# A third query tile, output weights split ahead of time, and later turning of weights in a two-layer streaming encoder

## The chip, the cores and the metric

The kernel runs on one core of a Trainium2 chip. The metric is the device time of one execution in microseconds (us); lower is better. The tensor engine (PE) multiplies, the vector (DVE), scalar (ACT) and GpSimd (POOL) engines do everything elementwise, and the sync engine (SP) issues nearly all DMAs, in the order of its own queue.

## What is computed

A prompt of 2048 frames and a sample of 64 frames with caches, model width 1024, 16 heads of 64. Layer one: RMSNorm, one projection to q, k, v and gate, softmax attention over a band of nine chunks of 64 frames, gate, output projection, residual. Then one shared k and v for layer two: stick-breaking attention (strictly causal, a running product instead of a softmax), gate, output projection, residual, final RMSNorm.

```python
# layer one, per chunk of 64 queries
s = einsum(q, k) * SCALE + rel_bias;  p = softmax(where(mask, s, NEG_INF));  o = p @ v
xp = xp + (o * silu(gate)) @ w_out_a
# layer two, per block of 128 queries, over all earlier keys
z = einsum(q, k) * SCALE
log_fail = where(mask, log_sigmoid(-z), 0)
later = flip(cumsum(flip(log_fail))) - log_fail
w = where(mask, exp(log_sigmoid(z) + later), 0);  o = w @ v
xp = xp + (o * silu(gate)) @ w_out_b
y = rms_norm(xp, norm_f)
```

## The kernel before, in words

Everything is float32. To keep precision on PE, an operand is split in a high part `hi` (rounded, on ACT) and the rest `lo` (on DVE), and a product is made of two or three matmuls: the helper `split`. Nearly every instruction is issued through one recording helper, so the profile gives them line L90; here they are told apart by the tiles they write and read.

The program has four stages, one after the other.

1. First projections (`projections("a", ...)`): `ps_v` and `ps_t` are their PSUM tiles. Beside them a list of small *stages* runs, a few per job: caches are turned and split and put into DRAM in the layout that the attention wants.
2. First attention, in *beats* (class `Beat`). One beat makes the scores `z` of one query tile of 128; two beats after the last tile of an item (`LAG["a"]`) its weights `s` are turned on PE (`wt`), split into `ph` and `pl`, and one beat later (`HOLD`) multiplied with v into `acc`. Between the beats, at `RATE` 0.4 steps a beat, goes work that fills PE: late projection jobs (`ps_j`, for the second half of the prompt), the splitting of the output weights (`w_out_steps`, which gives PE nothing), the output projection (`ps_o`).
3. Second projections, with stages of their own (`staged_b`): differences of v, and cached keys `kr` that are turned, split to `kh`, `kl` and stored in `k_b`.
4. Second attention, in beats again, `LAG` 5, `HOLD` 2, `RATE` 0.3. ACT makes `f` from `z`, POOL makes products of pairs (`two`), DVE scans them into `s` tiles (10 of them), POOL fills in the values between, then PE turns them. Per pair of heads the first half of the items has four query loads `q` (groups 1 and 0, two heads each): items of 8, 8, 4 and 4 beats, and a sample item of 2. `q` has two buffers, `kt` and `vt` (keys and values) five each.

In the beats most instructions aren't pinned: a scheduler at build time decides the place of each in its engine's queue, from the order in which the program gives them, buffers and its own estimate of times. Loads go through `Queue.load`, which makes a load stand behind the oldest store that was given at least 24 beats before it:

```python
behind = self.stores and self.stores[0][0] <= self.clock - self.pace
with tc.issue_after(self.stores[0][1].ins) if behind else nullcontext():
    nc.sync.dma_start(out, in_)
```

In a late k job of the first attention, `out` splits a chunk into `sp` and stores it (`k_a`), `add_back` adds the two parts on POOL into `lkn`, and `token_rows` turns `lkn` on PE (`ps_r`) for the output. `sp` and `lkn` share two buffers.

Of the kernel before, what the change touches and what calls it, by code (L numbers as in the profile page):

```python
# [9 lines left out]
F32 = mybir.dt.float32  # L10
F32R = mybir.dt.float32r
# [5 lines left out]
P = 128  # L17
D = 1024
NK = D // P
# [13 lines left out]
CH = 512  # L33
# [9 lines left out]
KEPT = "b"  # L43

RATE = dict(a=0.4, b=0.3)
LAG = dict(a=2, b=5)

LEAD = dict(a=8, b=14)
HOLD = dict(a=1, b=2)
# [21 lines left out]
def f32(ap):  # L71
    return ap.bitcast(F32)
# [28 lines left out]
def encoder_step(ctx: ExitStack, tc: tile.TileContext, a: dict, o: dict):  # L101
    nc = tc.nc
# [4 lines left out]
    def in_place(what):  # L107


        def pinned():  # L110
            was, order.on = order.on, order.amid
            what()
            order.on = was

        return pinned

    sp = order.engine(nc.sync)

    class Queue:


        def __init__(self, pace):
            self.pace, self.clock, self.stores = pace, 0, []

        def store(self, out, in_):
            self.stores.append((self.clock, nc.sync.dma_start(out, in_)))
# [1 line left out]
        def load(self, out, in_):  # L128
            while len(self.stores) > 1 and self.stores[1][0] <= self.clock - self.pace:
                self.stores.pop(0)  # L130
            behind = self.stores and self.stores[0][0] <= self.clock - self.pace
            with tc.issue_after(self.stores[0][1].ins) if behind else nullcontext():
                nc.sync.dma_start(out, in_)  # L133

# [3 lines left out]
    queue = Queue(24)  # L138
# [16 lines left out]
    def big_pair():  # L155
        return [big.tile([P, NK, D], F32R, name=f"big{i}", tag=f"big{i}") for i in range(2)]
# [28 lines left out]

    vraw = dram.tile([1 + T, D], F32, name="v_raw")
    x1d = dram.tile([T, D], F32, name="x1")
    biasd = [dram.tile([P, 2, 640], F32, name=f"bias_{i}") for i in range(HP)]
    relx = dram.tile([H, 384], F32, name="relx")

# [15 lines left out]
    def split(hi, lo, src):  # L206
        act.activation(hi, src, AF.Copy)
        dve.tensor_tensor(lo, src, f32(hi), ALU.subtract)
# [271 lines left out]
        nc.sync.dma_start(f32(lay["b"]["v"][to : to + n, heads]), f32(vs[:n]).rearrange("p h s d -> p h (s d)"))  # L480


    def stage_bias(hp, pool):
        for h in range(2):
            toe = pool.tile([P, 256], F32, name="toe", tag="toe", bufs=1)
            row = relx[2 * hp + h : 2 * hp + h + 1, 1:257]
            nc.sync.dma_start(toe, bass.AP(tensor=row.tensor, offset=row.offset, ap=[[1, P], [1, 256]]))
            bt = pool.tile([P, 640], F32, name="bt", tag="bt", bufs=1)
            dve.tensor_scalar(bt[:, 384:640], toe[:, ::-1], 8.0, None, ALU.mult)

            dve.tensor_scalar(bt[:, 0:384], toe[:, 255:256].to_broadcast([P, 384]), 8.0, None, ALU.mult)
            dve.memset(bt[DH:P, 0:DH], NEG8)
            dve.memset(bt[0:DH, 640 - DH : 640], NEG8)
            nc.sync.dma_start(biasd[hp][:, h], bt)
# [15 lines left out]
    def load_q(L, pool, hp, h, q0):  # L510

        there(L, "q", hp, q0)
        q = pool.tile([P, 2, CH], F32R, name="q", tag="q", bufs=3 if L == "a" else 2)
        src = f32(lay[L]["q"][hp][:, h * DH : h * DH + DH, place(q0) : place(q0) + CH]).rearrange("s d t -> d s t")
        for s in range(2):
            queue.load(f32(q[s * DH : s * DH + DH]), src[:, s : s + 2])
        return q
# [206 lines left out]
    def late_job(L, kind, w, c0, g, hp, x2, first, prompt):  # L724
        st = {}

        def load():
            if L not in KEPT:
                st["raw"] = opool.tile([P, NK, P], F32, name="lraw", tag="og", bufs=1)
                c = c0 + hp * P  # L730
                sp.dma_start(st["raw"], w[:, c : c + P].rearrange("(k p) c -> p k c", p=P))
            st["wh"] = opool.tile([P, NK, P], F32R, name="lwh", tag="oh", bufs=2)
            st["wl"] = opool.tile([P, NK, P], F32R, name="lwl", tag="ol", bufs=2)
            if L in KEPT:
                for i, part in enumerate((st["wh"], st["wl"])):
                    sp.dma_start(f32(part), f32(lay[L]["w"][kind, hp][i]))

        def cut(k0):
            ks = slice(k0, k0 + STEP)
            scaled_split(st["wh"][:, ks], st["wl"][:, ks], st["raw"][:, ks], g[:, ks])  # L740

        def some(c, k0):
            if k0 == 0:
                st["ps"] = bank("ps_j")
            ps, wh, wl = st["ps"], st["wh"], st["wl"]
            cols = slice(c, c + CH)
            for k in range(k0, k0 + STEP):
                mm(ps, wh[:, k], x2[0][:, k, cols], start=(k == 0), stop=False)
                mm(ps, wh[:, k], x2[1][:, k, cols], start=False, stop=False)
                mm(ps, wl[:, k], x2[0][:, k, cols], start=False, stop=(k == NK - 1))  # L750

        def out(c):
            ps = st["ps"]
            at = slice(place(HALF + c), place(HALF + c) + CH)
            if kind == "g":
                sg = opool.tile([P, CH], F32, name="sg", tag="xr", bufs=2)
                act.activation(sg, ps, AF.Sigmoid)
                dve.tensor_tensor(sg, ps, sg, ALU.mult)
                queue.store(lay[L]["g"][hp][:, at], sg)
            else:  # L760
                sp = opool.tile([P, 2, CH], F32R, name="sp", tag="xr", bufs=2)
                split(sp[:, 0], sp[:, 1], ps)
                for s in range(2):
                    put(L, kind, hp, s, at, sp[:, s], queue.store)
                st[c] = sp
            if c + CH == HALF:
                done_late.add((L, kind, hp))

        def add_back(c):

            st["kn"] = opool.tile([P, 2, CH], F32, name="lkn", tag="xr", bufs=2)
            gps.tensor_tensor(st["kn"][:, 0], f32(st[c][:, 0]), f32(st[c][:, 1]), ALU.add)

        def token_rows(c):
            kn = st["kn"]
            ps = bank("ps_r")
            for j in range(4):
                flip(ps[:, j * P : j * P + P], kn[:, 0, j * P : j * P + P])
            act.activation(kn[:, 1], ps, AF.Copy)
            b = HALF + c - first  # L780
            dst = prompt[b : b + CH, hp * P : hp * P + P]
            queue.store(dst.rearrange("(j p) c -> p j c", p=P), kn[:, 1].rearrange("p (j c) -> p j c", j=4))

        chunks = range(0, HALF, CH)
        behind = []
        for c in chunks:
            rows = kind == "k" and HALF + c >= first
            behind.append([partial(out, c)] + ([partial(add_back, c), (2, partial(token_rows, c))] if rows else []))
        products = [partial(some, c, k0) for c in chunks for k0 in range(0, NK, STEP)]
        cuts = [] if L in KEPT else [partial(cut, k0) for k0 in range(0, NK, STEP)]  # L790
        return [in_place(x) for x in [load] + cuts], products, behind

    def w_out_steps(src, w):

        raws = {}

        def load(k):
            if k < NK:
                tag = ("oh", "ol")[k % 2]
                raws[k] = opool.tile([P, D], F32, name="woraw", tag=tag, bufs=2)  # L800
                sp.dma_start(raws[k], src[k * P : (k + 1) * P])

        def cut(k):
            if k == 0:
                w.extend(big_pair())
            for c in range(0, D, CH):
                cols = slice(c, c + CH)
                split(w[0][:, k, cols], w[1][:, k, cols], raws[k][:, cols])
            del raws[k]

        return [
            (
                [in_place(partial(load, i)) for i in range(3)] if k == 0 else [],
                [None],
                [[in_place(partial(cut, k)), in_place(partial(load, k + 3))]],
            )
            for k in range(NK)
        ]
# [225 lines left out]
    staged_b = []  # L1044
    for i, (t, half) in enumerate((t, half) for t in range(len(TOK)) for half in range(2)):
        staged_b += [partial(stage_diff, "new", t, half), *keys_b[8 + i : 9 + i]]
    jobs_a = [("k", w_a, D, gs["a"]), ("q", w_a, 0, gs["a"]), ("g", w_a, 3 * D, gs["a"])]
    x2 = projections(
        "a",
# [15 lines left out]
    with (  # L1065
# [5 lines left out]
        KV, SB = 4, 9  # L1071
# [169 lines left out]
    with (  # L1241
# [15 lines left out]
            dve.tensor_scalar(dms[rows], own_s[rows, CH - P :][:, rows], NEGZ, None, ALU.mult)  # L1257
        own = psum.tile([P, CH], F32, name="own")
        dve.tensor_copy(own, own_s)
        KV, SB = 5, 10  # L1260
        banks.update(ph=4)

        ends["b"] = wpool.tile([P, HP, len(TOK)], F32, name="ends")
# [21 lines left out]
        beat = Beat(LAG["b"], HOLD["b"], False, 1.0)  # L1285
        beat.beside = job_steps("b", jobs_b, x2, 0, o["b_k_p"])
        beat.beside.insert(1, end_values())
        beat.beside += w_out_steps(a["w_out_b"][0], w_out)
        order.on = False
        gf = wpool.tile([P, D], F32, name="gf")  # L1290
        nc.sync.dma_start(gf, a["norm_f"].partition_broadcast(P))
# [179 lines left out]
            return [partial(one, c) for c in cs], [pack(i) for i in range(len(packs))]  # L1471

        beat.rate = RATE["b"]
        todo = items()
        first = next(todo)
        beat.lead(LEAD["b"])
# [46 lines left out]
```

## Time and profile before

| what | value |
| --- | --- |
| time, median of 3 runs | 3299.82 us |
| lowest and highest run | 3290.64, 3308.87 us |
| the profiled execution | 3298.24 us |
| its span, first to last instruction | 3296.4 us |
| mean granted clock of PE over it | 0.996 of full speed |
| first and second projections, roughly | 0 to 665 and 1305 to 2015 us |
| first and second attention with their output projections, roughly | 665 to 1305 and 2015 to 3297 us |

How to read it: the span is what the trace covers; 1.8 us of the profiled execution lie around it. The stages' limits are read from the windows of the trace. A granted clock of 1.00 means 2.4 GHz, and a stretch at 0.5 would be at 1.2 GHz throughout.

### The profile page before, as it was taken

How to read it: one execution, taken by the hardware profiler on the slowest of the kernel's cores; microseconds unless marked ns; L12 is line 12 of the kernel's file. 1: busy time of each engine (PE TensorE's matmuls, PEld its weight loads, DVE VectorE, ACT ScalarE, POOL GpSimd, SP SyncE). 2: the span in 40 equal slices, each digit the busy share in tenths (PEclk: the TensorE clock that was granted, in tenths of full speed). 3: DMA queues.
4: the chain of work that ended last, by engine and by line, in shares of the span. 5: the costliest groups of instructions: out<-in, count | busy, mean ns of one | idle time of the engine just before them, and what ended most of it. 6: DMA issues, size and time to landing. Idle time of an engine off the chain costs nothing.

```text
span 3296.4 us, 53612 instructions
## 1 busy us (share of the span) xinstructions
PE 3209.2 (97%) x17928; PEld 2789.1 (85%) x17928; DVE 1890.7 (57%) x3786; ACT 1712.6 (52%) x3719; POOL 1299.4 (39%) x1950
## 2 busy tenths in 40 slices
PE   8999999999999999999999999999999999999999
PEld 7889999988888998878899998887788877887877
DVE  4235431157778775231144333787778888888873
ACT  5234222258888775142243433665566666666662
POOL 3001110035655553020044101444367777777761
PEclk9999999999999999999999999999999999999999
DMA  6359992387899884453499988777745564455423
GB/s 205 116 195 363 352 332 109 121 244 222 228 272 271 236 244 140 136 188 116 148 372 339 322 291 281 205 202 192 205 125 154 161 180 134 129 146 139 128 90 118
DMA packets 457081, 671.62 MB, mean 204 GB/s; under 512 B 50805, under 2 KB 260757, under 8 KB 456806
## 3 DMA queue, kind: packets, MB, share of 16 engines
q1 hardware_dynamic: 397350, 617.07, 60.0%
q10 hardware_dynamic: 59456, 51.13, 4.8%
q8 instruction: 143, 2.34, 0.3%
q14 instruction: 132, 1.08, 0.1%
HBM read 400.39 MB, written 267.68 MB: 203 GB/s over the span
## 4 chain that ended last, share of the span: by engine, by line
PE 76%; issue 8%; DMA 6%; DVE 6%; ACT 3%; SPq 1%; POOL 1%; POOLq 0%; ACTq 0%; DVEq 0%
PE ps_t L90 24%; PE ps_v L90 11%; PE acc L90 10%; PE z L90 9%; PE wt L90 8%; PE ps_j L90 6%; PE ps_o L90 5%; DVE s L90 2%; DVE pl L90 2%; DMA q<-q_b 2%; SPq L133 1%; DMA kt<-k_b 1%; ACT ph L90 1%; PE ps_tr L90 1%; DMA vt<-v_b 1%
## 5 line engine op out<-in xcount | busy, mean ns | idle before, releaser
L90 DVE TENSOR_TENSOR pl<-wt,ph 128x512 fp32r<-128x512 f32 (+1 forms) x864 | 552.9, 654 | 126.7 <-ACT ph L90 123.1
L90 ACT ACTIVATE ph<-wt 128x512 fp32r<-128x512 f32 (+1 forms) x864 | 485.2, 577 | 188.5 <-PE wt L90 167.8
L90 PE MATMUL ps_t<-x_own,wh 128*128 128x362 f32 (+1 forms) x2304 | 569.0, 327 | 0.0
L90 PE MATMUL wt<-ident,s 128*128 128x128 f32 x3472 | 551.4, 274 | 12.9 <-DVE pl L90 6.4
L90 PEld LDWEIGHTS wt<-ident,s 128*128 128x128 f32 x3472 | 420.0, 141 | 90.6 <-DVE pl L90 12.2
L90 ACT ACTIVATE f<-z 128x512 f32<-128x512 f32 (+4 forms) x680 | 356.5, 535 | 224.0 <-PE z L90 162.5
L90 PEld LDWEIGHTS ps_t<-x_own,wh 128*128 128x128 f32 x2304 | 405.3, 188 | 1.8
L90 POOL TENSOR_TENSOR s<-f,s 128x256 f32<-128x256 f32 x416 | 362.0, 871 | 108.5 <-DVE s L90 103.4
L90 PE MATMUL z<-kt,q 128*128 128x512 f32 (+3 forms) x1280 | 376.2, 381 | 24.9 <-DMA q<-q_b 19.8
L90 PE MATMUL acc<-ph,vt 128*128 128x512 f32 (+3 forms) x1088 | 375.1, 379 | 3.8 <-ACT ph L90 3.1
L90 PE MATMUL ps_t<-x_own,wl 128*128 128x362 f32 (+1 forms) x1152 | 376.4, 327 | 0.0
L90 PE MATMUL acc<-pl,vt 128*128 128x512 f32 (+3 forms) x1088 | 363.4, 367 | 13.1 <-DVE pl L90 12.4
L90 POOL TENSOR_SCALAR s<-s,rc 128x640 f32<-128x640 f32 (+5 forms) x264 | 199.8, 764 | 374.3 <-DMA keys<-k_a 194.6
L90 PE MATMUL ps_o<-big,oh 128*128 128x512 f32 x1088 | 336.5, 392 | 2.2 <-ACT oh L90 2.2
L90 DVE TENSOR_TENSOR_SCAN s<-two,s,own 128x256 f32<-128x256 f32 x408 | 299.7, 738 | 44.5 <-POOL two L90 32.9
L90 POOL TENSOR_TENSOR two<-f 128x256 f32<-128x256 f32 x416 | 259.3, 625 | 129.9 <-ACT f L90 119.5
L90 PEld LDWEIGHTS z<-kt,q 128*128 128x128 f32 x1280 | 221.7, 192 | 58.5 <-issue 19.2
L90 PE MATMUL ps_j<-big,lwh 128*128 128x512 f32 x768 | 248.9, 399 | 1.3 <-DVE pp L90 0.8
L90 PE MATMUL ps_t<-big,wh 128*128 128x512 f32 x768 | 238.6, 391 | 0.0
L90 PEld LDWEIGHTS ps_o<-big,oh 128*128 128x128 f32 x1088 | 201.9, 188 | 43.3 <-ACT oh L90 2.6
L90 PEld LDWEIGHTS acc<-pl,vt 128*128 128x128 f32 x1088 | 194.4, 190 | 47.3 <-DVE pl L90 31.1
L90 DVE TENSOR_TENSOR_SCAN s<-f,own 128x128 f32<-128x128 f32 (+4 forms) x264 | 202.9, 788 | 46.2 <-ACT f L90 42.8
(146 smaller groups left out, 5522.0 us busy)
## 6 DMA issues: line engine op xcount, KB each, us to landing
vt<-v_b SPq DMA_DIRECT2D x80, 512.0 KB, 6.7
v_b<-vs SPq DMA_DIRECT2D x64, 512.0 KB, 6.1
q<-q_a SPq DMA_DIRECT2D x128, 256.0 KB, 5.8
q<-q_b SPq DMA_DIRECT2D x128, 256.0 KB, 4.3
vt<-v_a SPq DMA_DIRECT2D x48, 512.0 KB, 6.6
kt<-k_b SPq DMA_DIRECT2D x96, 256.0 KB, 6.7
keys<-k_a SPq DMA_DIRECT2D x80, 256.0 KB, 7.0
v_a<-vs ACTq DMA_DIRECT2D x32, 512.0 KB, 2.8
```

The costliest lines, as they stand in the source:

```text
L90: ins = op(*args, **kwargs)
L133: nc.sync.dma_start(out, in_)
```

## The change

Six edits, one of them a new stage:

- `LAG["a"]` 2 to 3: in the first attention the weights of an item are turned one beat later.
- `add_back` is given two steps after `out` and `token_rows` four, instead of one after the other with two steps before `token_rows`.
- `w_out_b` (the second output weights) is loaded and split in the stages of the second projections (`stage_w_out`, 16 of them) and stored in DRAM (`wod`); in the second attention the halves are loaded straight into the `big` tiles instead of raw weights being loaded and split there.
- `q` has three buffers in the second attention too.
- `SB` 10 to 12 there: twelve `s` tiles.
- `queue.until = 40`: after beat 40 of the second attention loads need not stand behind stores.

```diff
-LAG = dict(a=2, b=5)
+LAG = dict(a=3, b=5)
...
-            behind = self.stores and self.stores[0][0] <= self.clock - self.pace
+            behind = self.stores and self.stores[0][0] <= self.clock - self.pace and self.clock < self.until
...
+    wod = [dram.tile([P, 2, D], F32R, name=f"wo_{k}") for k in range(NK)]
...
+    def stage_w_out(k, half, pool):
+        raw = pool.tile([P, CH], F32, name="vcur", tag="vr", bufs=2)
+        cols = slice(half * CH, half * CH + CH)
+        nc.sync.dma_start(raw, a["w_out_b"][0][k * P : (k + 1) * P, cols])
+        vs = pool.tile([P, 2, CH], F32R, name="vs", tag="vs", bufs=2)
+        split(vs[:, 0], vs[:, 1], raw)
+        nc.sync.dma_start(f32(wod[k][:, :, cols]), f32(vs))
...
-        q = pool.tile([P, 2, CH], F32R, name="q", tag="q", bufs=3 if L == "a" else 2)
+        q = pool.tile([P, 2, CH], F32R, name="q", tag="q", bufs=3)
...
-            behind.append([partial(out, c)] + ([partial(add_back, c), (2, partial(token_rows, c))] if rows else []))
+            behind.append([partial(out, c)] + ([(2, partial(add_back, c)), (4, partial(token_rows, c))] if rows else []))
...
+        def parts(k):
+            if k == 0:
+                w.extend(big_pair())
+            for i in range(2):
+                sp.dma_start(f32(w[i][:, k]), f32(wod[k][:, i]))
+
+        if src is None:
+            return [([], [None], [[in_place(partial(parts, k))]]) for k in range(NK)]
...
+    staged_b += [partial(stage_w_out, k, half) for k in range(NK) for half in range(2)]
...
-        KV, SB = 5, 10
+        KV, SB = 5, 12
...
-        beat.beside += w_out_steps(a["w_out_b"][0], w_out)
+        beat.beside += w_out_steps(None, w_out)
...
+        queue.until = 40
```

What the scheduler makes of it is seen in the engines' queues. SP in the second attention, one pair of heads (the seventh) in the first half, before: `o_b` is a store of attention output, `gate_b` and `q_b<-sp` are stores of late jobs, `lwh` and `lwl` their weights, `qs` and the small `kt` and `vt` belong to the sample.

```order
L90 DMA lwh<-w_bg_145 128x1024
L90 DMA lwl<-w_bg_145 128x1024
L126 DMA gate_b_131<-sg 128x512
L133 DMA q<-q_b_116 64x2x512 x2
L133 DMA q<-q_b_117 64x2x512 x2
L126 DMA q_b_114<-sp 128x512 x3
L133 DMA q<-q_b_117 64x2x512 x2
L126 DMA o_b_137<-ot 128x512
L133 DMA gt<-gate_b_134 128x512
L133 DMA qs_21281<-q_b_117 64x2x64 x2
L133 DMA kt<-k_b_125 128x2x64
L133 DMA q<-q_b_117 64x2x512 x2
```

The same place of SP's queue after the change:

```order
L90 DMA lwh<-w_bg_145 128x1024
L90 DMA lwl<-w_bg_145 128x1024
L127 DMA gate_b_131<-sg 128x512
L134 DMA kt<-k_b_125 128x2x512
L134 DMA q<-q_b_117 64x2x512 x4
L134 DMA vt<-v_b 128x4x256
L127 DMA q_b_114<-sp 128x512 x3
L134 DMA q<-q_b_117 64x2x512 x2
L134 DMA kt<-k_b_126 64x2x512 x4
L134 DMA kt<-k_b_126 128x2x64
L134 DMA qs_21387<-q_b_113 64x2x64 x2
L127 DMA o_b_137<-ot 128x512
```

Against the same store of the gate the query loads stand one item further ahead (two of the seventh pair's come at once instead of one of the sixth's and one of the seventh's), and the keys of the eighth pair (`k_b_126`) now stand ahead of the output store.

SP near the end of the second projections, before (`q_b<-sh`, `sl` are the stores of a q job, `w_bq` keeps its split weights for the late job):

```order
L233 DMA q_b_114<-sh 128x1088 x2
L233 DMA q_b_114<-sl 128x1088
L380 DMA w_bq_154<-wh 128x1024
L380 DMA w_bq_154<-wl 128x1024
L233 DMA q_b_115<-sh 128x1088 x2
```

And after:

```order
L434 DMA kr<-in_cache_b_k 128x4x128
L236 DMA k_b_126<-kh 128x512
L236 DMA k_b_126<-kl 128x512
L236 DMA q_b_114<-sh 128x1088 x2
L236 DMA q_b_114<-sl 128x1088
L383 DMA w_bq_154<-wh 128x1024
L383 DMA w_bq_154<-wl 128x1024
L492 DMA wo_165<-vs 256x1x512
L489 DMA vcur<-in_w_out_b 128x512
L236 DMA q_b_115<-sh 128x1088 x2
```

The new loads and stores stand among the q jobs, and the staging of the cached keys, which had ended before, now reaches to the last q jobs.

POOL at the start of the first attention, after the last difference of v; these rows read the same before and after:

```order
L90 TENSOR_SCALAR s<-s,rc 128x640 x2
L90 TENSOR_TENSOR lkn<-sp 128x512
L90 TENSOR_SCALAR s<-s,rc 128x640 x6
L90 TENSOR_SCALAR s<-s,rc 128x128
L90 TENSOR_SCALAR s<-s,rc 128x256
```

Nothing moved there: the first `lkn` is still the third instruction, although the program gives it later. PE's queue is unchanged as well up to the first `ps_r`, which stands 16 rows later than before.

## Rows read from the trace of the kernel before

**Rows 1.** The page's busy times, the line of PE and the others

```profile
PE 3209.2 (97%) x17928; PEld 2789.1 (85%) x17928; DVE 1890.7 (57%) x3786; ACT 1712.6 (52%) x3719; POOL 1299.4 (39%) x1950
```

**Rows 2.** Windows by stage: length, busy us by engine, granted clock, DMA share, GB/s

```profile
665.00:1305.00 640.00, 616.24 (x3871) 548.55 (x3870) 461.70 (x1245) 485.82 (x1107) 335.95 (x384) 0.99 0.81 231
1305.00:1820.00 515.00, 514.25 (x2547) 438.58 (x2546) 154.38 (x264) 156.57 (x326) 110.75 (x101) 1.00 0.63 220
1820.00:2015.00 195.00, 195.00 (x1210) 194.48 (x1209) 63.37 (x167) 72.19 (x194) 9.45 (x8) 1.00 0.86 300
2015.00:2400.00 385.00, 358.96 (x2054) 303.62 (x2053) 286.82 (x475) 220.34 (x468) 158.92 (x274) 0.98 0.75 208
2400.00:2680.00 280.00, 277.81 (x1576) 231.61 (x1575) 222.91 (x353) 180.16 (x350) 198.21 (x375) 1.00 0.50 145
2680.00:2760.00 80.00, 72.23 (x403) 57.11 (x402) 74.23 (x119) 59.14 (x118) 61.34 (x103) 0.98 0.61 175
2760.00:3190.00 430.00, 419.79 (x2379) 345.57 (x2378) 370.17 (x590) 287.74 (x578) 329.88 (x601) 1.00 0.46 132
```

**Rows 3.** Waits of PE, 665 to 1305 us: total us, times, longest

```profile
PE z L90 <- DVE mn L90: 7.3, 12, 1.3
PE wt L90 <- POOL s L90: 4.9, 1, 4.9
```

**Rows 4.** Waits of PE, 2015 to 3297 us

```profile
PE z L90 <- DMA q<-q_b: 19.8, 8, 5.1
PE acc L90 <- DVE pl L90: 11.2, 28, 1.4
```

**Rows 5.** Windows of 20 us in which the granted clock was below 1.00

```profile
700.00:720.00 20.00, 16.32 (x102) 14.85 (x103) 12.64 (x41) 13.68 (x35) 10.38 (x15) 0.83 0.66 180
2060.00:2080.00 20.00, 16.72 (x93) 14.25 (x91) 13.16 (x20) 10.21 (x20) 1.14 (x4) 0.91 0.89 237
2280.00:2300.00 20.00, 18.68 (x97) 15.64 (x97) 13.73 (x23) 12.82 (x29) 5.59 (x10) 0.83 0.31 97
2320.00:2340.00 20.00, 16.98 (x94) 14.46 (x94) 12.34 (x20) 9.14 (x20) 2.44 (x5) 0.91 0.57 165
2360.00:2380.00 20.00, 16.75 (x88) 13.93 (x87) 12.85 (x21) 9.30 (x19) 4.94 (x9) 0.91 0.92 267
```

**Rows 6.** Timeline of POOL: start, us, instruction, idle time before and its releaser

```profile
701.31 1.26 POOL L90 TENSOR_TENSOR lkn<-sp 128x512 f32<-128x512 f32 x1 [7.83 <-DMA k_a<-sp]
```

**Rows 7.** Timeline of PE just after

```profile
703.41 0.69 PE L90 MATMUL wt<-ident,s 128*128 128x128 f32 x2 [4.86 <-POOL s L90]
```

**Rows 8.** Waits of SP's queue, 2005 to 2400 us, by the line that issues

```profile
SPq L133 <- PE z L90: 36.2, 15, 8.3
SPq L126 <- DVE ot L90: 25.8, 8, 4.0
```

**Rows 9.** The chain that ended last: start, us, what (query loads)

```profile
2271.56 9.58 DMA q<-q_b
...
2320.14 8.39 DMA q<-q_b
...
2365.23 9.26 DMA q<-q_b
```

**Rows 10.** The tile q in the second attention: issue to landing of its loads

```profile
DMA to landing us min/median/max: 3.5/4.3/11.2
```

**Rows 11.** The tile woraw, 2600 to 2800 us: duration ns min/median/max, first and last start

```profile
L90 ACT ACTIVATE big<-woraw x16: 613/622/653, 2693.8 to 2736.9; 128x512 fp32r<-128x512 f32 x16
L90 DVE TENSOR_TENSOR big<-woraw,big x16: 659/679/1352, 2695.3 to 2739.9; 128x512 fp32r<-128x512 f32 x16
```

**Rows 12.** Waits of DVE, 2040 to 3200 us

```profile
DVE s L90 <- PE wt L90: 12.7, 7, 4.0
```

**Rows 13.** Windows of 10 us at the start of the second attention

```profile
2020.00:2030.00 10.00, 9.49 (x47) 7.34 (x45) 1.20 (x2) 1.37 (x3) 0.00 (x0) 1.00 1.03 304
2060.00:2070.00 10.00, 7.93 (x45) 6.63 (x43) 6.35 (x9) 4.36 (x8) 0.67 (x1) 1.00 1.08 270
```

More of the change, by code (lines that the diff above doesn't have):

```diff
@@ L122, in __init__ @@
         def __init__(self, pace):
-            self.pace, self.clock, self.stores = pace, 0, []
+            self.pace, self.clock, self.stores, self.until = pace, 0, [], 10**6
         def store(self, out, in_):
```

## The prediction

> **What bounds the kernel now.** I read the page first. PE is busy 97% of the span, every other engine far less [rows 1]: PE sets the time. The change adds no matmul and takes none away (before and after hold the same 17928, shape by shape), so it can win only time in which PE stands still or runs at half its clock, 87 us of idle time in all (3296.4 - 3209.2), and lose by making more of it.
>
> The windows by stage say where that time lies [rows 2]. The second projections leave PE nothing: 195.00 busy of 195, and 0.75 idle in the 515 before. The first attention has 23.8 us idle of 640, the start of the second 26.0 of 385, then 2.2 of 280, 7.8 of the 80 from 2680, and 10.2 of the 430 behind. In the stretch of the 7.8 DVE is 93% busy.
>
> Then the waits of PE: which of them answers to an edit. In the second attention the largest is the query load, 19.8 us in 8 waits [rows 4]. In the first it is DVE's softmax minimum, 7.3 us in 12 small waits, and one wait of 4.9 us for weights that POOL still has to scale [rows 3].
>
> Last the granted clock. It is 1.00 almost everywhere, and below it in the slices around or behind a stall [rows 5]. A mean of 0.83 over 20 us is work lost for (1 - 0.83) x 20 = 3.4 us; 0.91 is 1.8 us. The four slices of the second attention make 1.8 + 3.4 + 1.8 + 1.8 = 8.8 us. [...]
>
> **The third query tile.** SP stands 36.2 us between 2005 and 2400, 15 times, before a load that needs a buffer which PE's scores still read, and 25.8 us before stores whose data DVE hasn't made [rows 8]. The query loads end waits on the chain every 46 to 49 us (2271.56, 2320.14, 2365.23) [rows 9]: once per pair of heads. A pair is 8 + 8 + 4 + 4 + 2 = 26 beats, so a beat is some 1.8 us. With two buffers the fourth query tile of a pair can be loaded only when the second's item has ended, one item of 4 beats (7 us) ahead of need, and the first of the next pair 6 beats (11 us) ahead; a load takes up to 11.2 us from issue to landing [rows 10], and 8.4 to 9.6 on the chain [rows 9]. With three buffers the shortest lead is 10 beats, 18 us, longer than any load of before. So the buffer is the cause of the repeating wait, and the third one ends it. In SP's new queue the query loads do stand earlier, and `until` lets the keys of the next pair pass the output store; both help. At stake is 19.8 + 8.8 = 28.6 us. The two earliest waits lie where the DMA engines are full anyway (share 1.03 and 1.08) [rows 13], and there a buffer does not make a transfer faster. I take 23; the bounds are 0 (all late for other reasons) and 28.6.
>
> **The output weights.** In the second attention 16 splits go: 16 x 0.622 us on ACT and 16 x 0.679 on DVE, 10.0 and 10.9 us, between 2694 and 2740 [rows 11]. On ACT that is slack. On DVE it is not: in the 80 us around, DVE is busy 74.2, and PE idles 7.8 us and loses (1 - 0.98) x 80 = 1.6 us of clock [rows 2]. The stretch before idles 2.2 in 280, or 0.6 in 80, so at most 7.8 + 1.6 - 0.6 = 8.8 us come back. The eight empty steps, in which PE gets no filling work, stay, since the new list has them too, and without filling work a beat is tight on DVE and POOL as well (61.3 of the 80 us). I take 6, bounds 0 and 8.8. The loads that replace the raw ones are twice the bytes (16 of 512 KB for 8), at a DMA share of 0.61 there: covered, and each has steps of three beats before it is used.
>
> **What they cost in the second projections.** Per stage one ACT and one DVE split of the same size: about 10 and 11 us where ACT and DVE are busy 72.2 and 63.4 of 195 us [rows 2]; PE's full queue covers them. The DMAs are the question. Sixteen stages load 0.26 and store 0.52 MB each, 12.6 MB, on SP, among the stores of the q jobs. From 1820 to 2015 the share is 0.86 at 300 GB/s: 58.5 MB moved, and a full share would be 300 / 0.86 = 349 GB/s, 68 MB. The new total is 71.1 MB, 204 us of transfers for 195 us of matmuls, so about 9 us spill into the next stage's first loads, if nothing else gives. What is behind SP there is the weights of the first late jobs, then the first queries and keys. The earlier stretch (share 0.63 over 515) has a little room, since of the now 74 stages for 24 jobs the first two jobs carry four each. I take a loss of 4; bounds 0 and 9 plus a halved clock of 3.4, 12.4. By the Trainium skill (Perfetto Trace Analysis, section Roofline) a single active core is bounded by its 16 DMA engines at about 435 GB/s; by that figure the stretch could carry 84.8 MB, all would fit, and the sum below would be lower by the 4. The trace's own ratio (349) is what I go by.
>
> **The later turn and the later add.** The 4.9 us wait at 703 comes from POOL: it stood 7.8 us before `lkn` until a store of `k_a` had landed [rows 6], and the weights behind it in its queue were late for PE [rows 7]. With the 3.4 us of clock [rows 5] it costs 8.3. The diff reads as its cure, since `lkn` is given later. But the scheduler, which thinks the buffer free, put the first `lkn` at the same place of POOL's queue, ahead of the same weights, and PE's queue is the same up to there. So this wait stays. For the rest of the stage one beat more only helps where PE waits for finished weights, and that was this one wait; the 12 waits for DVE [rows 3] are scores that want a PSUM buffer, which no edit touches. The stage ends with one beat more to drain, under output products that fill PE. I take a gain of 2 for the changed order; bounds: a gain of 8.3, and a loss of 2.4, a beat of this stage (640 us over 264 beats: 16 tiles of 16 pair-and-half rounds and 8 samples).
>
> **Twelve `s` tiles** answer DVE's 12.7 us before tiles that PE still turns [rows 12]. DVE is off the path nearly everywhere, except where it is 93% busy, and there its waits are others. Nothing; bounds a gain of 5 (under half of it) and a loss of 5 from a changed mix of turns and products.
>
> **The sum.** 3298.2 (the profiled execution: its span and 1.8 us around) - 23 - 6 + 4 - 2 = 3271 us. The median of the runs is 1.6 us above that execution, so the two bases agree. A change by under 0.5% (16.5 us: 3283.3 to 3316.3) is about what a measurement of this kernel cannot tell from none.
>
> **The rivals.**
> The query loads stay late: SP is one queue, and a load in it waits not only for its own buffer but for every store ahead of it (25.8 us for DVE's `ot` alone [rows 8]); the new queue has two query loads in a row, of which the second can block keys and values behind it. For it: stores do stop SP. Against: the period of the waits and their size fit the buffer. Then a third of the 28.6 comes back: 3298.2 - 9.5 - 6 + 4 = 3287, no change that can be told.
>
> Slower, by one mechanism: the end of the second projections becomes bound by DMA. Its place is 1820 to 2015, its price 71.1 MB / rate - 195 us. To pass 3316.3 from 3271 it must cost 45 us above the 4 I took, 244 us in all, which is 291 GB/s. Rates of 304 and 270 at a full share do occur, in the loads of queries and keys at the start of the second attention [rows 13]; against it stands the stretch itself, 300 GB/s at 0.86. It decides from some 290 GB/s downward.
>
> More than forecast: PE's busy time hides short waits, as ends of matmuls are modelled. The Trainium skill (Perfetto Trace Analysis, Identifying the Most-Contended Engine) says that matmul busy time is no good measure of the distance to the limit, and to look at weight loads instead; those are at 85% [rows 1]. If the edits free PE of waits inside the 97%, all upper bounds together give 3298.2 - 28.6 - 8.8 - 8.3 - 5 = 3247, with nothing lost in the projections.
>
> That single edits do nothing is in the sum already: the first wait of the first attention and the twelve tiles.
>
> **How the numbers follow.** The forecast 0.69, late loads anyway 0.16, DMA-bound projections 0.07, more than forecast 0.08. The forecast's own bounds go from 3250 to some 3290, mostly under 3283: 0.61 of its 0.69 is faster, 0.08 the same. Faster 0.61 + 0.08 = 0.69, same 0.08 + 0.16 = 0.24, slower 0.07. The range goes from 3247 to 3292, which takes in the first rival and leaves out the slow one.
>
> **What would show it.** Right: the query wait of PE in the second attention under 6 us, with no slice under 1.00 between 2100 and 2400; the 80 us with the empty steps near 1 to 3 us idle and no split of `big`; the wait for `lkn` in the first attention still there; PE still 195 of 195 in the end of the second projections at a share near 1. Wrong: idle PE before `ps_t` or at the first `ps_j`, or a new wait for `kt` or `vt` in place of `q`. The weakest step is how far the 12.6 MB spill over, and next to it the order that the scheduler made of thousands of instructions, of which I read only places.

## The result and the profile after

The changed kernel takes 3278.45 us, the median of 6 runs (3274.95 to 3280.43); the kernel before took 3300.09 us beside it (3290.64 to 3308.87). The ratio is 0.9931 [0.9918, 0.9944], so it is faster by 0.7%. The forecast was 3271 us. The profiled execution took 3280.0 us (span 3278.2).

The page's busy times of the changed kernel, to be read against [rows 1]:

```profile
PE 3204.2 (98%) x17928; PEld 2791.0 (85%) x17928; DVE 1887.0 (58%) x3786; ACT 1711.4 (52%) x3719; POOL 1291.4 (39%) x1950
```

PE's matmuls are the same in number. The windows by stage of the changed kernel, as in [rows 2]: length, busy us by engine (PE, PEld, DVE, ACT, POOL), granted clock, DMA share, GB/s:

```profile
665.00:1305.00 640.00, 616.50 (x3876) 550.16 (x3875) 463.14 (x1246) 484.26 (x1107) 335.58 (x384) 0.99 0.81 230
1820.00:2015.00 195.00, 195.00 (x1209) 194.07 (x1208) 73.31 (x176) 80.41 (x211) 12.93 (x11) 1.00 0.98 352
2015.00:2100.00 85.00, 74.54 (x374) 62.41 (x373) 46.25 (x76) 34.12 (x70) 23.07 (x44) 0.92 0.98 270
2100.00:2400.00 300.00, 297.11 (x1777) 253.55 (x1777) 254.01 (x425) 196.22 (x420) 146.78 (x253) 1.00 0.75 214
2680.00:2760.00 80.00, 71.03 (x389) 59.01 (x388) 63.62 (x100) 48.66 (x96) 54.84 (x100) 0.91 0.65 213
```

The same view of the kernel before, with the start of the second attention cut as it is above:

```profile
2015.00:2100.00 85.00, 77.58 (x422) 64.83 (x421) 50.05 (x82) 40.20 (x83) 26.90 (x49) 0.98 0.90 257
2100.00:2400.00 300.00, 281.38 (x1633) 238.78 (x1632) 236.78 (x394) 180.15 (x385) 132.03 (x225) 0.98 0.71 194
```

Three stretches differ most. From 2100 to 2400 PE's idle time falls from 18.6 to 2.9 us and its clock goes back to 1.00: here the time comes from. From 2015 to 2100 idle time grows from 7.4 to 10.5 us, at a clock of 0.92 instead of 0.98. And the 80 us from 2680 are no better: 9.0 us idle where 7.8 were [rows 2], and a clock of 0.91 where 0.98 was, although DVE there has fallen from 74.2 to 63.6 us. (These windows lie at fixed times, and the faster kernel is ahead of the slower. Cut by the program instead, from 60 us before the first `ps_o` of the stage to 20 behind it, the idle time is 7.8 us before and 8.8 after, so the reading stands.)

The waits of PE from 2000 us to the end, as in [rows 4] (waiting instruction, releaser: total us, times, longest):

```profile
PE acc L90 <- DMA vt<-v_b: 7.5, 2, 5.3
...
PE z L90 <- DMA q<-q_b: 5.8, 2, 3.6
```

The query wait has gone from 19.8 us in 8 to 5.8 us in 2, and these two lie ahead of 2100: from 2100 to 2400 no query load ends a wait of PE. In its place stands a wait for values, `vt`, that the kernel before did not have. The chain that ended last shows where it lies (start, us, what; the load that ends it lands at 2702.8):

```profile
2684.24 8.95 DMA vt<-v_b
...
2693.26 9.51 DMA vt<-v_b
```

In the same place the DMA loads, from 2660 to 2710 us (KB each, median us from issue to landing), and the line of SP's queue (packets, MB, share of the 16 engines):

```profile
big<-wo SPq DMA_DIRECT2D x16, 512.0 KB, 8.9
vt<-v_b SPq DMA_DIRECT2D x6, 512.0 KB, 9.8
...
q1 hardware_dynamic: 8616, 15.24, 98.4%
```

All sixteen loads of split output weights are issued in these 50 us, 8.4 MB through one queue, and a load of `vt` lands after 9.8 us (the median of six). Over the whole second attention its median is 4.8:

```profile
DMA to landing us min/median/max: 2.3/4.8/12.4
```

SP's timeline shows the order (start, us, loads in a row; L134 is the ordered load): between two loads of values stand five loads of weights, and single loads of keys, of `og` and of a residual row (`xr`).

```profile
2669.55 0.53 SPq L134 DMA_DIRECT2D vt<-v_b  x1
2670.16 0.58 SPq L134 DMA_DIRECT2D kt<-k_b  x1
2671.37 5.55 SPq L90 DMA_DIRECT2D big<-wo  x5
2678.22 0.37 SPq L90 DMA_DIRECT2D og<-o_b  x1
2680.47 3.68 SPq L90 DMA_DIRECT2D xr<-x  x1
2684.24 1.93 SPq L134 DMA_DIRECT2D vt<-v_b  x1
```

Eight of the sixteen are issued ahead of the load at 2684.24, the first that PE waits for. SP had also stood still for 7.9 us just ahead of the first of them, until PE's late projections (`ps_j`) let go of the buffer; the values stand behind that too:

```profile
SPq L90 <- PE ps_j L90: 7.9, 1, 7.9
```

In the first attention POOL still waits ahead of `lkn`, and PE behind it; the two lines answer to [rows 6, 7]:

```profile
702.41 1.26 POOL L90 TENSOR_TENSOR lkn<-sp 128x512 f32<-128x512 f32 x1 [7.65 <-DMA k_a<-sp]
```

```profile
704.50 0.69 PE L90 MATMUL wt<-ident,s 128*128 128x128 f32 x2 [4.66 <-POOL s L90]
```

### The profile page after: what moved, and what is told of

Read it like the earlier page. It is cut to its first block, busy times and chain, and to the rows that moved or that the text cites. A ratio compares the mean times of both kernels' runs of the same rounds, so it can differ in the third digit from the quotient of the medians.

```text
span 3278.2 us, 53687 instructions
## 1 busy us (share of the span) xinstructions
PE 3204.2 (98%) x17928; PEld 2791.0 (85%) x17928; DVE 1887.0 (58%) x3786; ACT 1711.4 (52%) x3719; POOL 1291.4 (39%) x1950
## 4 chain that ended last, share of the span: by engine, by line
PE 75%; issue 7%; DVE 6%; DMA 6%; ACT 2%; POOL 2%; SPq 1%; POOLq 0%; ACTq 0%; DVEq 0%
PE ps_t L90 23%; PE ps_v L90 11%; PE acc L90 10%; PE z L90 9%; PE wt L90 8%; PE ps_j L90 6%; PE ps_o L90 5%; DVE s L90 3%; DVE pl L90 2%; DMA vt<-v_b 1%; PE ps_tr L90 1%; ACT ph L90 1%; DMA kt<-k_b 1%; POOL s L90 1%; ACT s L90 1%
## 5 line engine op out<-in xcount | busy, mean ns | idle before, releaser
L90 PEld LDWEIGHTS acc<-ph,vt 128*128 128x128 f32 x1088 | 198.7, 192 | 37.1 <-ACT ot L90 8.4
L90 DVE CUSTOM_DVE_ANT_0 s<-z,bias 128x640 f32<-128x640 f32 (+4 forms) x256 | 184.7, 733 | 77.2 <-PE wt L90 51.1
```

The lines of the kernel that those rows point to most:

```text
L90: ins = op(*args, **kwargs)
```

## The experiments

Ratios are against the kernel before, with a 95% interval, the runs of both taken on one chip. Beside them I give a **stretch**: the time from the first `ps_j` of the second attention to the first `ps_o` behind it, read from the one profiled execution. It is 722.9 us before and 705.6 after. It leaves out the first attention and the projections, whose end moved by up to 10.7 us between executions of the same instructions (last section). Two kernels below, the later turn alone and the last one, differ from the kernel before and from the change without the stored weights only ahead of the stretch; in it their instructions stand in the same order, but for one matmul in the last. Yet it is 725.1 us against 722.9, and 701.7 against 698.1. So a difference under some 4 us says nothing.

**The third query tile alone,** on the kernel before:

```
-        q = pool.tile([P, 2, CH], F32R, name="q", tag="q", bufs=3 if L == "a" else 2)
+        q = pool.tile([P, 2, CH], F32R, name="q", tag="q", bufs=3)
```

> The kernel before with a third query tile alone. If the buffer is what made the query loads late, PE's wait for q in the second attention falls from 19.8 us to under 8 and the time to about 3300 - 20 = 3280 us. If the loads are late because they must stand behind stores (the edit of `until` is needed), or because the transfers are slow, the wait stays above 15 us and the time stays within 3300 +- 6.

Measured: 3278.58 us, 0.9945 [0.993, 0.9961], stretch 694.8. The query wait is one of 1.4 us:

```profile
PE z L90 <- DMA q<-q_b: 1.4, 1, 1.4
```

From 2100 to 2400 PE is as full as in the whole change:

```profile
2100.00:2400.00 300.00, 296.89 (x1762) 252.55 (x1761) 252.01 (x419) 193.49 (x412) 146.69 (x254) 1.00 0.75 207
```

One edit of one number gives most of the gain of all.

**The stored output weights alone,** on the kernel before:

```
+    staged_b += [partial(stage_w_out, k, half) for k in range(NK) for half in range(2)]
...
-        beat.beside += w_out_steps(a["w_out_b"][0], w_out)
+        beat.beside += w_out_steps(None, w_out)
```

(with `wod`, `stage_w_out` and `parts` as in the change.)

> The kernel before with the stored output weights alone. Theory: the relief of DVE is eaten by 8.4 MB of loads that SP issues ahead of values (PE waits for vt near 2690 us, 7 us and as much again of half clock) and by the spill at the end of the second projections: 3300 + 3 us (-3 to +12). Rival: the relief is worth its 6 to 9 us and the wait for vt comes from something else: 3292 us.

Measured: 3303.49 us, 1.0012 [1.0, 1.0025], stretch 718.9. No gain. In the 80 us DVE falls from 74.2 to 68.2, and PE's idle time from 7.8 to 5.7:

```profile
2680.00:2760.00 80.00, 74.33 (x425) 61.16 (x424) 68.16 (x110) 54.80 (x108) 58.53 (x111) 0.98 0.77 252
```

Against that the start of the second attention loses: 75.91 busy at a clock of 0.92, where 77.58 at 0.98 was.

```profile
2015.00:2100.00 85.00, 75.91 (x383) 62.56 (x382) 44.88 (x76) 33.50 (x69) 20.08 (x39) 0.92 0.97 273
```

The time is as expected, but one half of its reason is not: PE never waits for `vt` here. So the stored weights do not make that wait by themselves; it takes other edits beside them.

**The change without the third query tile:**

```
-        q = pool.tile([P, 2, CH], F32R, name="q", tag="q", bufs=3)
+        q = pool.tile([P, 2, CH], F32R, name="q", tag="q", bufs=3 if L == "a" else 2)
```

> The changed kernel with two query tiles again. If the third tile carries the gain, PE's wait for q is back at 15 to 25 us and the time is 3278 + 18 = 3296 us; if `until` and the order do, 3280 us.

Measured: 3280.43 us, 0.9954 [0.9938, 0.9969], stretch 704.0. The query wait hardly comes back:

```profile
PE z L90 <- DMA q<-q_b: 6.5, 3, 5.0
```

So something else in the change removes the same wait. SP's waits from 2100 to 2400 in this kernel, and how long its query loads take there:

```profile
SPq L134 <- PE z L90: 61.9, 21, 6.5
...
SPq L127 <- POOL s L90: 14.6, 7, 2.7
SPq L127 <- DVE sg L90: 10.8, 5, 3.4
...
DMA to landing us min/median/max: 3.6/4.3/7.1
```

and the same in the kernel before:

```profile
SPq L133 <- PE z L90: 26.0, 11, 8.3
SPq L126 <- DVE ot L90: 25.8, 8, 4.0
SPq L126 <- POOL s L90: 24.4, 9, 3.4
SPq L126 <- DVE sg L90: 18.1, 3, 7.8
...
DMA to landing us min/median/max: 3.5/4.5/10.4
```

(L126 and L127 issue a store, L133 and L134 a load.) SP now stands less before stores and more before loads that wait for a buffer: it is there early, and issues as soon as PE lets go. A query load then lands after at most 7.1 us, where the kernel before had 10.4. (The wait for `vt` is 3.2 us here.)

**The change without the stored weights:**

```
-        beat.beside += w_out_steps(None, w_out)
+        beat.beside += w_out_steps(a["w_out_b"][0], w_out)
```

and no staging.

> The changed kernel with the output weights loaded raw and split in the second attention as before. Theory: the wait for vt near 2690 us and the full DMA at the start of the second attention go, DVE's stall of 8 us near 2700 comes back: 3278 - 5 = 3273 us (3266 to 3280). Rival (the stored weights are part of the gain): 3284 us or more.

Measured: 3272.25 us, 0.9926 [0.991, 0.9942], stretch 698.1. The ratio cannot be told from that of the whole change; the stretch is 7.5 us shorter. There is no wait for `vt`, and at the start of the second attention PE loses no more than in the kernel before:

```profile
2015.00:2100.00 85.00, 78.03 (x425) 65.32 (x424) 52.79 (x86) 41.75 (x86) 28.77 (x53) 0.98 0.98 273
2680.00:2760.00 80.00, 75.21 (x392) 58.91 (x393) 73.50 (x113) 57.09 (x112) 62.43 (x105) 0.96 0.41 124
```

**`until` alone,** on the kernel before: from beat 40 a load may pass the oldest store.

```
-            behind = self.stores and self.stores[0][0] <= self.clock - self.pace
+            behind = self.stores and self.stores[0][0] <= self.clock - self.pace and self.clock < self.until
...
+        queue.until = 40
```

> The kernel before, in which loads need not stand behind stores after beat 40 of the second attention, and nothing else. If this edit and the third query tile are two cures of one wait, PE's wait for q falls under 9 us here too and the time is about 3300 - 14 = 3285 us; if e3 came out fast for another reason (order, twelve tiles, lag), the wait stays at 20 us and the time at 3297 us.

Measured: 3282.79 us, 0.9947 [0.9929, 0.9965], stretch 702.2. The query wait is gone here too, but for 5.1 us that lie ahead of 2100:

```profile
PE z L90 <- DMA q<-q_b: 5.1, 2, 3.1
```

**The change without both:**

```
-        q = pool.tile([P, 2, CH], F32R, name="q", tag="q", bufs=3)
+        q = pool.tile([P, 2, CH], F32R, name="q", tag="q", bufs=3 if L == "a" else 2)
...
-        queue.until = 40
```

> The changed kernel with two query tiles and with loads behind stores, so with the stored weights, the lag of three, the later add and the twelve tiles alone. Two cures of one wait: PE's wait for q is back at 15 to 25 us and the time at 3300 us (3292 to 3306). Another cause: 3282 us.

Measured: 3296.71 us, 0.9988 [0.9973, 1.0004], stretch 718.7. The wait is back, and with it nearly the whole time:

```profile
PE z L90 <- DMA q<-q_b: 17.1, 8, 4.7
```

All other edits together are worth nothing that can be told. (Of the wait for `vt`, 2.4 us are left.)

**Staged earlier:** the sixteen stages go into the first projections.

```
-    staged_b += [partial(stage_w_out, k, half) for k in range(NK) for half in range(2)]
+    staged += [partial(stage_w_out, k, half) for k in range(NK) for half in range(2)]
```

> The changed kernel with the sixteen weight stages among those of the first projections, where the DMA share is 0.64. If the spill of these transfers out of the second projections makes the start of the second attention slow, its first quarter falls from 286 us to about 278 and the time by 7 us, to 3271; if the start is slow because of the order of its own loads, nothing changes (3278).

Measured: 3270.96 us, 0.991 [0.9892, 0.9929], stretch 698.8. The end of the second projections has its old share of DMA, and the second attention starts with less loss:

```profile
1820.00:2015.00 195.00, 195.00 (x1206) 193.89 (x1205) 63.60 (x167) 72.21 (x194) 11.00 (x9) 1.00 0.85 298
2015.00:2100.00 85.00, 78.54 (x410) 66.10 (x410) 47.12 (x76) 36.32 (x76) 26.01 (x47) 0.94 0.97 266
```

The wait for `vt` stays, 6.7 us in 2, as it should: the loads of weights ahead of it were not touched. So does SP's stand of 7.9 us.

**Behind the values:** the loads of split weights are issued only behind the last load of `vt` that the program has given by then.

```
-                sp.dma_start(f32(w[i][:, k]), f32(wod[k][:, i]))
+                with tc.issue_after(queue.values.ins):
+                    sp.dma_start(f32(w[i][:, k]), f32(wod[k][:, i]))
```

(`queue.values` is what `queue.load` returned for `vt`.)

> The changed kernel in which each load of the stored weights stands behind the last load of values that the program has given. If the burst of weight loads makes PE wait for vt near 2690 us, that wait (7.5 us and 6.8 us of half clock) goes and the time is 3278 - 10 = 3268 us; if the values were late for their buffers, it stays and the time too.

Measured: 3272.86 us, 0.9916 [0.9897, 0.9934], stretch 696.8. The interval overlaps that of the whole change; the stretch is 8.8 us shorter. No wait for `vt` is left, and the 80 us are at full clock with 3.0 us idle:

```profile
2680.00:2760.00 80.00, 77.03 (x432) 62.09 (x431) 70.86 (x111) 55.02 (x109) 62.55 (x116) 1.00 0.70 224
```

The edit takes away two things at once: the weights ahead of the values, and SP's stand of 7.9 us ahead of the weights, which is not in this kernel. The long waits for `vt` (6.7 to 7.8 us) are in kernels that have both, the short ones (2.4 and 3.2 us) in two that have the weights without the stand, and a third such kernel, the stored weights alone, has none. Which of the two makes how much of the wait was not separated.

**The addition in order:** `add_back` is held behind the last scaling of the soft-max in POOL's queue.

```
+            with tc.issue_after(queue.scaled.ins):
                 gps.tensor_tensor(st["kn"][:, 0], f32(st[c][:, 0]), f32(st[c][:, 1]), ALU.add)
```

(`queue.scaled` is the last `gps.tensor_scalar(s, s, rc, ...)`.)

> The changed kernel with the first addition of a late k job held behind the last scaling of weights that the program gave before it, so that POOL does five more scalings before it. Theory: PE's wait of 4.7 us near 704 us is POOL standing in front of that addition; it goes, with up to 3.4 us of half clock: 3278 - 7 = 3271 us. Rival: the data of the next scores is as late, and another wait takes its place: 3278 us.

Measured: 3282.08 us, 0.9937 [0.9918, 0.9956], stretch 707.1: no gain, as the rival had it. The 20 us around the old wait are now full, and POOL reaches `lkn` with no idle time before it:

```profile
700.00:720.00 20.00, 20.00 (x130) 17.77 (x129) 15.65 (x48) 16.39 (x42) 10.39 (x15) 1.00 0.97 261
```

```profile
703.82 1.30 POOL L90 TENSOR_TENSOR lkn<-sp 128x512 f32<-128x512 f32 x1
```

Yet PE's busy time in the first attention is 616.97 of 640, after 616.50 in the whole change. The waits of PE in that stage show where the rest went:

```profile
PE acc L90 <- ACT ot L90: 8.9, 9, 4.8
...
PE acc L90 <- DVE pl L90: 4.2, 5, 1.7
```

In the whole change the first of them was 5.6 us and the last 0.7. A wait was removed, and as far as one execution of each shows, the stage gave it back later.

**Only the later turn,** on the kernel before:

```
-LAG = dict(a=2, b=5)
+LAG = dict(a=3, b=5)
```

> The kernel before with the lag of three beats in the first attention alone. Theory: PE hardly waits there for finished weights, so nothing: 3298 (3293 to 3303). Rival: one beat more of room takes the small waits too: 3298 - 10 us.

Measured: 3300.45 us, 0.9994 [0.9978, 1.0011], stretch 725.1. The wait of 4.9 us for POOL is still there.

**All three mended:** staged earlier, behind the values, the addition in order, on the whole change (the edits of the three runs above).

> The changed kernel with the weight stages in the first projections, the weight loads behind the values, and the addition in order. If the three waits are apart from each other the gains of e7, e8 and e9 add: 3278 - 7 - 6 - 6 = 3259 us. If the time is then set by other waits in their place: 3268 us or more.

Measured: 3267.90 us, 0.9892 [0.9872, 0.9911], stretch 685.9. This kernel is faster than the one before and clear of the interval of the whole change. It is not the 3259 us of three gains added: against the ratio of the whole change the first two edits gave 0.21 and 0.15%, the third nothing, and the three together 0.39%. The start of the second attention and the 80 us are mended at once:

```profile
2015.00:2100.00 85.00, 79.69 (x443) 68.02 (x442) 47.58 (x78) 36.91 (x78) 25.98 (x47) 1.00 0.98 275
2680.00:2760.00 80.00, 77.10 (x426) 61.98 (x425) 70.67 (x111) 53.49 (x106) 62.60 (x117) 1.00 0.71 224
```

**Without stored weights, with the addition in order:** the edits of two runs above together.

> As e4 (no stored weights), with the addition in order. If staging ahead is worth having once its two costs are mended, this is slower than e11 by DVE's stall near 2700 us, some 6 to 9 us: 3272 - 6 = 3266 us. If it is not, the two are equal within 3 us.

Measured: 3274.59 us, 0.9914 [0.9894, 0.9934], stretch 701.7. This can't be told from the change without the stored weights, so the addition in order gives nothing here either. What the run was for is the comparison with the one above, which has the stored weights and was taken beside it: 6.7 us slower (3271.22 to 3283.66 against 3264.06 to 3268.48), with a stretch 15.8 us longer. That is the side on which staging ahead is worth having once its two costs are mended. One wait for `vt` of 2.9 us, at 2685, is in this kernel too, without any stored weights; the values have other causes to be late.

## Why the prediction was right, and where its terms were off

The forecast was a gain, from the query loads, and that is what came: 3278 us measured for 3271 forecast, inside the range. By the stretch the excess of some 7 us lies in one item, the output weights: all the rest of the change gives 24.8 us (722.9 to 698.1; forecast 23), and the stored weights take 7.5 back where the forecast had a gain of 2 (6 less the 4 that they cost). Two of the signs that the forecast had named went against it, both here: a new wait for `vt` came, and the 80 us were 9.0 us idle instead of 1 to 3.

**The third query tile (forecast 23, bounds 0 to 28.6).** From 2100 to 2400 the idle time of PE fell by 15.7 us (18.6 to 2.9) and the clock rose from 0.98 to 1.00, up to 6.0 us more; by itself the third tile shortens the stretch by 28.1 us and the runs by 0.55%, 18 us. The mechanism and its size hold, and so does what was to show it: a query wait under 6 us (5.8), and 1.00 for the clock from 2100 to 2400. The two waits that are left lie ahead of 2100, where the forecast had said that a buffer would not help. But "the buffer is the cause of the repeating wait" is only half of it. `until` alone removes the same wait with two buffers. With both undone it returns. A query load was late because its buffer came free late **and** because SP, when it did, was standing before a store. Either cure is enough: with two buffers and `until`, the load lands 7.1 us after issue at most from 2100 to 2400, and some 7 us is what the forecast had worked out as the shortest lead of two buffers. The forecast's "both help" is right for each alone (0.55% and 0.53%), and wrong for the two as a sum: together with all the rest they make 0.69%. The rival that the loads stay late behind stores named the right second cause, but not that the change removes it as well.

**The output weights (forecast 6, bounds 0 to 8.8).** This is the step that failed: "at a DMA share of 0.61 there: covered". The relief of DVE is real: with the loads behind the values, the idle time of PE in the 80 us falls from 7.8 to 3.0 us, at the top of the 1 to 3 that the forecast named. (Cut by the first `ps_o`, it is 2.6 us, and 6.4 in the change without the stored weights.) But a mean share over 80 us says nothing of the order in one queue. The scheduler put eight of the sixteen loads of 512 KB, and SP's stand of 7.9 us before them, ahead of values that were wanted at once; PE waited 7.5 us for `vt`, and the clock fell in the first of the two waits. So in the whole change the term was a loss of some 7 us (1.2 us more of idle time, and up to 5.6 of clock) instead of a gain of 6. In the run of the stored weights alone, without that wait, it was a gain of 2.1 us of idle time. The Trainium skill (DMA: Bandwidth & Descriptors, section Queues, rings and completion order) says that each DMA engine takes the descriptors of a queue in ring order; the trace agrees, in that the loads of `vt` issued among the bulk landed after 9.8 us and not 4.8 (medians), with SP's queue taking 98.4% of the engines.

**The end of the second projections (forecast a loss of 4, bounds 0 to 12.4).** The share went to 0.98 at 352 GB/s, and PE stayed at 195.00 of 195: as forecast, the loss is not there but behind. Its size shows over all kernels. By the windows from 2015 to 2100, some of them shown above: in the six that stage the weights at the end (the change, the second, third and sixth run, the two with loads behind the values and with the addition in order) PE is idle 9.1 to 13.1 us of the 85 from 2015, at a clock of 0.92 to 0.96. In the six that stage none (the kernel before, and the runs with the third tile, `until`, or the later turn alone and the two without stored weights) it is idle 3.4 to 7.4 us, at 0.96 to 1.00. The two that stage earlier lie at 6.5 and 5.3. The middles of the two sixes are 11.9 and 7.0 us, so the staging costs some 5 us, and by the clock up to 4 more (their middles are 0.93 and 0.98, of 85 us). The term of 4 was small, and its bound of 12.4 held. The Trainium skill gives about 435 GB/s as what bounds a single active core (Perfetto Trace Analysis, section Roofline); this mix of loads and stores stayed below that, with 352 GB/s at a share of 0.98, so here the trace's own ratio of rate to share was the better basis. Whether the bytes or the place of the stages in SP's queue makes the loss was not separated.

**The later turn and the later add (forecast 2).** That the wait at 703 stays because the scheduler puts `lkn` at the same place was right (4.66 us). `LAG` alone gave nothing that can be told (0.9994), though an interval of some 11 us cannot exclude 2; the later add was not run alone. The upper bound of 8.3 was too high for a second reason: when the wait was really removed, no time was won (0.9937 against 0.9931 of the whole change, 0.9914 against 0.9926 without the stored weights), and PE waited for `ot` and `pl` in other places instead. By these waits that stage is held by several engines in turn, not by the one wait.

**Twelve tiles** were never run alone; with the later turn, the later add and the stored weights they make 0.9988, nothing that can be told. The traces show a little more. DVE's wait for turned tiles, 12.7 us before [rows 12], is 11.6 to 13.5 us in all five kernels with ten tiles and is in none of the nine with twelve. PE's idle time from 2760 to 3190 is 9.5 to 10.2 us in the five and 7.4 to 8.2 in the nine. So some 2 us may come from there, inside the forecast's bounds and too little for the runs to tell.

**The sum.** By the stretch, the third tile alone gives 28.1 us and `until` alone 20.7, and the stored weights take 7.5 back. Mending the two places where they do (stages earlier, loads behind the values), with the addition in order, which gave nothing by itself, brought 3267.9, below the forecast and clear of the change's own interval; each mend alone was too small for its interval to tell. Sums of idle time and clock over a stretch are upper bounds, since the low clock in part lies on the idle time itself.

**Two readings of the forecast** were off and carry no weight: the query loads of [rows 9] start 45 and 49 us apart, not 46 to 49; and the first of the two earliest query waits ended at 2056.5, outside the window 2020 to 2030 of [rows 13]. The DMA share from 2050 to 2060 was 1.04, so what was concluded from it stands.

## What to carry to other kernels

When a load is late, ask of both its buffer and its place in the queue, and undo each edit alone and both together: two cures of one wait do not add up. Work that is taken off a busy engine and comes back as bulk loads has moved into a queue; place it behind the loads that are wanted at once, and read the order that the scheduler made, not the order of the code. Here it then paid: 6.7 us against the same kernel without the stored weights. A mean DMA share of 0.65 over 80 us hid 30 us at a full share.

## What was not expected of the hardware

**Executions differ by ten microseconds in a stage whose instructions are the same.** Up to the first `ps_v` of the second projections, the kernel before and three of the runs (third tile, stored weights, `until`, each alone) show the same instructions in the same order on each engine, and yet that `ps_v` starts at 1416.9, 1422.6, 1420.9 and 1427.6 us in one execution of each. A difference under 10.7 us up to there, read from one execution of each kernel, shows nothing; this is why the stretch was used above, and it limits what the addition in order could show.

**A stall costs more than its idle time.** Around the two waits for `vt`, in windows of 10 us of the changed kernel, the granted clock goes to 0.54:

```profile
2680.00:2690.00 10.00, 6.93 (x50) 5.68 (x48) 8.63 (x16) 5.16 (x11) 9.41 (x17) 0.95 1.04 379
2690.00:2700.00 10.00, 6.76 (x28) 5.97 (x29) 4.02 (x6) 3.86 (x7) 4.58 (x11) 0.54 1.07 314
2700.00:2710.00 10.00, 7.84 (x35) 6.15 (x35) 6.15 (x10) 4.80 (x10) 4.10 (x9) 0.83 1.06 389
```

From 2690 to 2700 that is nearly the lower of its two levels (1.2 of 2.4 GHz). Of this window PE was idle only 3.2 us, the end of a wait that had begun at 2687.9 and was 5.3 us long; the rest of the loss is the clock. The same two matmuls take 0.73 us ahead of that wait and 1.20 behind it:

```profile
2687.19 0.73 PE L90 MATMUL z<-kt,q 128*128 128x512 f32 x2 [1.00 <-ACT f L90]
2693.24 0.80 PE L90 MATMUL acc<-ph,vt 128*128 128x512 f32 x1 [5.31 <-DMA vt<-v_b]
...
2696.46 1.20 PE L90 MATMUL z<-kt,q 128*128 128x512 f32 x2
...
2702.81 0.79 PE L90 MATMUL acc<-ph,vt 128*128 128x512 f32 x1 [2.16 <-DMA vt<-v_b]
```

The second wait, of 2.2 us, came with a lower clock too: 0.83 from 2700 to 2710.
